# Two-layer encoder: layer 1's feature tiles by seven quarter products, attention without bias tiles, and an empty list of moves

## The chip, the cores and the metric

The kernel runs on one core of a Trainium2 chip (trn2). The metric is the time of one execution on the device, in microseconds; several runs are taken and the median is used. The engines are called PE (matmul), PEld (weight load), DVE (VectorE), ACT (ScalarE), POOL (GpSimd) and SP (the queue that issues most DMAs).

## The reference

The input is 1024 tokens of 1024 features, in float32. Layer 0 has two groups of dense attention (8 heads A, 8 heads B); layer 1, which the change touches, has banded attention. Each layer ends in an output product and a gated residual add. What matters here, cut from the reference (`C_Q` = 1024, `C_KV` = 256, 16 query heads in 4 groups, head size 64, `WINDOW` = 128):

```python
def odd_mixer(h, w_in, sink, w_out, slopes):
    proj = h @ w_in
    qc, kc, vc, gc = jnp.split(proj, [C_Q, C_Q + C_KV, C_Q + 2 * C_KV], axis=-1)
    oc = windowed_sink_attention(qc, kc, vc, sink, slopes)
    return (oc * jax.nn.silu(gc)) @ w_out

# inside windowed_sink_attention, per block of 128 queries and its 3 blocks of keys
bias = -slopes * jnp.abs(rel)
sc = jnp.einsum('bnqkgd,bnskd->bnkgqs', qb, kb) * scale + bias      # -inf outside the band
m = jnp.maximum(jnp.max(sc, axis=-1, keepdims=True), sink_l)
p = jnp.exp(sc - m)
denom = jnp.sum(p, axis=-1, keepdims=True) + jnp.exp(sink_l - m)
```

## The kernel before

Every matmul is done as three: each operand is split into a high part (rounded to the format that PE multiplies fast) and a low part (the rest), and high x high, high x low and low x high are added in PSUM (`mm3`, line 705). So each operand needs a cast (ACT or POOL) and a subtraction (DVE or POOL).

**The order of the work.** The kernel's text does not issue instructions; it records operations in a `Recorder`. A list scheduler (`run`, line 319) then goes through them with a duration for each operation and latencies between engines, and puts on each engine, whenever it is free, the recorded operation with the best priority whose operands are ready and whose buffers can be had. SBUF tiles of 128x1024 float32 come from one pool of `U_BUFS` = 49. `rec.at(shift=...)` lowers a priority, so that filler work goes where nothing else is ready. The list's order is then altered by `MOVES` (line 73), 359 entries of the form (kind, i, j): kind 0 puts operation i, with what it depends on, ahead of j; kind 1 puts i, with what depends on it, behind j (`moved`, line 549). The result is the fixed order in which each engine works.

**The stages,** by the time at which they run in the profiled execution: the input products (to 139 us), heads A in 16 groups with the gate tiles as filler (to 414), heads B in 16 groups (to 642), layer 0's output product and then the entrance of layer 1 (to 759), 32 windows of banded attention with layer 1's feature tiles as filler (to 1053), layer 1's output product (to the end). Groups of heads are numbered 0 to 31, and side work is hung on a group's number: `WS_AT` places sums of weight quarters that DMAs form in DRAM (plain copies on SP, accumulating copies on POOL's queue), `ADA_AT` places blocks of the sums that form shift, scale and gate from the conditioning (`ada_sum`: a 512 KB load and a 128x1024 product-and-sum on DVE, four or eight to a block). The last two blocks stand in the output product of layer 0 (`("op", 1, 7)`) and in a window (`("w", 2, 2)`).

**The output products** of both layers use Winograd's form of Strassen's scheme (`wino_out`, line 1646): 2x2 blocks, seven products instead of eight.

**The feature tiles.** `proj_ft` (line 1847) multiplies one tile of 128 features (2 for keys, 8 for queries, 8 for gates) with one half of the tokens (512): 8 chunks of 128 inputs, three matmuls of 128x512 each, 24 per half. The modulated input of layer 1 lies in `hT1`, 16 tiles for high and low parts of both halves. `fill` takes the next half from a list; six stand ahead of the first window, the others among the windows. Each tile's weights are one load of 512 KB, split on POOL (`wload`, line 873).

**A window** (`win_S`, line 1932, and `win_PV`) takes four heads with the same keys: eight matmuls for the scores, then per head one DVE operation that adds a bias tile (`win_bias`, POOL, four tiles per group of windows) and takes the maximum with the sink's logit, an exponential on ACT with its sum, a division on POOL; between them three small DVE operations and a small exponential for the sink's share. Transposes, splits and the products with the values follow in the next window.

Of the kernel before, what the change touches and what calls it, by code (L numbers as in the profile page):

```python
# [19 lines left out]
P = 128  # L20
# [17 lines left out]
NTAB = 1920  # L38

U_BUFS = 49  # L40
# [29 lines left out]
ADA_AT = (8, 5, ("c2", 6), 2, 4, 10, ("op", 1, 7), ("w", 2, 2))  # L70


MOVES = (
# [60 lines left out]
)  # L134

SLOPES = [float(np.float32(2.0) ** np.float32(-8.0 * k / 16)) for k in range(1, 17)]


class VP:
# [495 lines left out]
def encoder_kernel(ctx: ExitStack, tc: tile.TileContext, xt, ada_t, w_c1, w_c2, w_c3, w_g0, w_uq, w_ukv, w_out0, w_v1,  # L635
# [1211 lines left out]
    def proj_ft(n, name, evac):  # L1847
# [5 lines left out]
        def half(b):  # L1853
            ps = PA(f"{name}{b}")
            for kc in range(KC):
                m_ = mm3(ps, st["w"][kc], hT1[b][kc], kc == 0, kc == KC - 1)
                if kc == 0:
                    first = m_
# [269 lines left out]
```

## Time and profile before

| what | value |
|---|---|
| runs | 1158.09, 1158.74, 1157.87 us; median 1158.09 |
| profiled execution | 1156.2 us from the first to the last instruction (its span; the page gives no other time of it) |
| PE busy | 1129.2 us, 6070 matmuls and transposes |
| DVE / ACT / POOL busy | 924.1 / 697.2 / 592.2 us |
| DMA | 137.64 MB, 119 GB/s on the mean |
| mean granted clock of PE | 0.995 of full speed |

The span is the profiled execution on the chip, first to last instruction; a run's time also holds what lies around that. Busy time of an engine is the time in which one of its instructions was running; matmuls overlap each other, so a busy PE is not yet a PE at its best pace.

### The profile page before, as it was taken

How to read it: one execution, taken by the hardware profiler on the slowest of the kernel's cores; microseconds unless marked ns; L12 is line 12 of the kernel's file. 1: busy time of each engine (PE TensorE's matmuls, PEld its weight loads, DVE VectorE, ACT ScalarE, POOL GpSimd, SP SyncE). 2: the span in 40 equal slices, each digit the busy share in tenths (PEclk: the TensorE clock that was granted, in tenths of full speed). 3: DMA queues.
4: the chain of work that ended last, by engine and by line, in shares of the span. 5: the costliest groups of instructions: out<-in, count | busy, mean ns of one | idle time of the engine just before them, and what ended most of it. 6: DMA issues, size and time to landing. Idle time of an engine off the chain costs nothing.

```text
span 1156.2 us, 17595 instructions
## 1 busy us (share of the span) xinstructions
PE 1129.2 (98%) x6070; PEld 955.9 (83%) x6070; DVE 924.1 (80%) x1662; ACT 697.2 (60%) x1406; POOL 592.2 (51%) x563
## 2 busy tenths in 40 slices
PE   7999999999999999999999999999999999999996
PEld 6898887777788978888888888988888888888885
DVE  7974899898888888888889996858876587766895
ACT  5543366665665787887789823328755466565623
POOL 1235388957875644433436445605465266345524
PEclk9999999999999999999999999999999999999998
DMA  9600466754563251331065335200002112046313
GB/s 367 267 1 30 176 220 199 200 166 153 149 176 92 71 154 51 94 82 50 25 175 209 134 128 191 102 19 19 19 19 92 55 56 92 19 154 247 128 37 146
DMA packets 44617, 137.64 MB, mean 119 GB/s; under 512 B 5488, under 2 KB 8048, under 8 KB 44528
## 3 DMA queue, kind: packets, MB, share of 16 engines
q1 hardware_dynamic: 41648, 127.08, 31.7%
q0 software_dynamic: 2304, 8.39, 4.1%
q8 instruction: 48, 0.79, 0.3%
q10 hardware_dynamic: 576, 1.05, 0.2%
q14 instruction: 41, 0.34, 0.1%
HBM read 105.43 MB, written 39.45 MB: 125 GB/s over the span
## 4 chain that ended last, share of the span: by engine, by line
PE 83%; ACT 4%; DVE 4%; issue 2%; POOL 1%; DMA 1%; SPq 0%; POOLq 0%; ACTq 0%; DVEq 0%
PE psum L612 83%; DVE nm L612 1%; ACT hla L612 1%; ACT Pb L612 1%; ACT Pa L612 1%; DVE hlb L612 1%; ACT hlb L612 1%; DVE hla L612 0%; DMA xr<-in_xt 0%; DVE p L612 0%; ACT q L612 0%; POOL r L612 0%; SPq L612 0%; DVE adag L612 0%; ACT p L612 0%
## 5 line engine op out<-in xcount | busy, mean ns | idle before, releaser
L612 DVE TENSOR_REDUCE nm<-psum 128x1 f32<-128x1024 f32 x128 | 155.1, 1218 | 15.1 <-PE psum L612 13.7
L612 POOL TENSOR_SCALAR p<-p,dn 128x384 f32<-128x384 f32 (+1 forms) x128 | 73.2, 591 | 160.1 <-ACT p L612 71.5
L612 POOL TENSOR_SCALAR Pa<-Pa,rs 128x1024 f32<-128x1024 f32 x64 | 77.0, 1210 | 45.1 <-DVE rs L612 39.6
L612 POOL TENSOR_SCALAR Pb<-Pb,rs 128x1024 f32<-128x1024 f32 x64 | 73.9, 1160 | 44.6 <-DVE rs L612 40.7
L612 PE MATMUL psum<-hla,VA 128*128 128x512 f32 x256 | 89.3, 417 | 3.5 <-DVE hla L612 2.8
L612 DVE TENSOR_TENSOR hla<-psum,hla 128x512 fp32r<-128x512 f32 x128 | 83.9, 683 | 10.6 <-ACT hla L612 10.1
L612 DVE TENSOR_TENSOR hlb<-psum,hlb 128x512 fp32r<-128x512 f32 x128 | 82.7, 684 | 8.9 <-ACT hlb L612 8.4
L612 ACT CAST hla<-psum 128x512 fp32r<-128x512 f32 x128 | 71.2, 594 | 26.9 <-PE psum L612 25.5
L612 PE MATMUL psum<-hlb,VB 128*128 128x512 f32 x256 | 87.3, 422 | 0.1
L612 ACT ACTIVATE Pa<-psum,nm 128x1024 f32<-128x1024 f32 x64 | 71.6, 1120 | 25.3 <-DVE nm L612 21.9
L612 PE MATMUL psum<-ident,Pa 128*128 128x128 f32 x512 | 85.7, 272 | 1.1 <-ACT Pa L612 0.6
L612 PE MATMUL psum<-k,q 128*128 128x512 f32 x256 | 84.1, 402 | 1.6 <-DMA k<-knp 1.1
L612 ACT ACTIVATE Pb<-psum,nm 128x1024 f32<-128x1024 f32 x64 | 71.9, 1124 | 21.0 <-DVE nm L612 14.9
L612 DVE CUSTOM_DVE_ANT_0 p<-psum,bias,rows_g 128x384 f32<-128x384 f32 (+1 forms) x128 | 69.9, 580 | 17.3 <-PE psum L612 16.4
L612 PE MATMUL psum<-ident,Pb 128*128 128x128 f32 x512 | 80.0, 272 | 0.4 <-DVE hlb L612 0.3
L612 ACT COPY ot<-psum 64x512 f32<-64x512 f32 x64 | 37.4, 585 | 69.6 <-PE psum L612 69.1
L612 ACT ACTIVATE p<-p,nm 128x384 f32<-128x384 f32 (+1 forms) x128 | 74.1, 587 | 1.5 <-DVE nm L612 1.5
L612 PEld LDWEIGHTS psum<-ident,Pa 128*128 128x128 f32 x512 | 63.7, 140 | 13.5 <-ACT Pa L612 1.0
L612 ACT CAST hlb<-psum 128x512 fp32r<-128x512 f32 x128 | 69.9, 602 | 5.4 <-PE psum L612 4.6
L612 PEld LDWEIGHTS psum<-ident,Pb 128*128 128x128 f32 x512 | 63.0, 140 | 11.4 <-issue 0.6
L612 ACT CAST hl<-psum 128x512 fp32r<-128x512 f32 x88 | 46.7, 592 | 29.4 <-PE psum L612 28.7
L612 DVE TENSOR_TENSOR hl<-psum,hl 128x512 fp32r<-128x512 f32 x88 | 56.1, 685 | 10.2 <-ACT hl L612 9.7
(891 smaller groups left out, 3596.5 us busy)
## 6 DMA issues: line engine op xcount, KB each, us to landing
ada<-in_ada_t SPq DMA_DIRECT2D x32, 512.0 KB, 7.4
ws<-in_w_out POOLq DMA_DIRECT2D x16, 512.0 KB, 7.3
adag<-in_ada_t SPq DMA_DIRECT2D x16, 512.0 KB, 4.2
S<-ws SPq DMA_DIRECT2D x16, 512.0 KB, 4.4
o<-spill SPq DMA_DIRECT2D x12, 512.0 KB, 5.0
A<-in_w_out SPq DMA_DIRECT2D x12, 512.0 KB, 5.5
xT<-in_xt SPq DMA_DIRECT2D x8, 512.0 KB, 8.4
ws<-in_w_out SPq DMA_DIRECT2D x8, 512.0 KB, 7.7
```

The lines of the kernel that those rows point to most:

```text
L612: fn(*[real(v) for v in a], **{k: real(v) for k, v in kw.items()})
```

## The change

Three things change together.

1. **Seven quarter products for a pair of feature tiles.** The 18 tiles are put in nine pairs (`F_PAIRS`). A pair's weights form a 2x2 of quarters (tile x half of the inputs), the inputs another (half of the inputs x half of the tokens). Four combinations of the weight quarters are formed in DRAM for all pairs, 18 steps at groups 14 to 31 (`feature_sums`: 12 plain copies and 12 accumulating ones of 768 KB). The right-hand combinations are formed once (`combined`) from a float32 copy of the modulated input that `modulate` now writes as well (`keep`), and split into high and low parts: seven operands of four tiles each. `f_step` does one quarter product: 4 chunks x 3 matmuls of 128x512, and what follows it (copies and sums of PSUM banks, or the evacuation of a finished half). Ten of the 63 steps stand ahead of the first window, 53 among the windows. Weights come as pairs of 256 KB quarters, split on POOL (`f_load`); quarter "3" is negated on ACT.
2. **Attention without bias tiles.** Queries are scaled by a power of two of their own and negated; the DVE operation of the scores then takes `relt` (two tables of 384 columns) directly, with a scale and a minimum. The sink's logit is written as one more column of the score tile by POOL, so the exponential's sum holds it. Gone are the bias tiles, the three small DVE operations and the sink's exponential.
3. **The order.** `MOVES` is empty. The last two `ADA_AT` blocks move to groups 18 and 22. `U_BUFS` is 52, and the space that the program reserves for POOL's DMA descriptors is set to 2048.

The diff, cut to its core:

```diff
-U_BUFS = 49
+U_BUFS = 52
-ADA_AT = (8, 5, ("c2", 6), 2, 4, 10, ("op", 1, 7), ("w", 2, 2))
+ADA_AT = (8, 5, ("c2", 6), 2, 4, 10, 18, 22)
-MOVES = (
-    (0, 711, 679), (1, 710, 624), (0, 79, 3), (1, 0, 48), (1, 13, 15), (1, 14, 13), (1, 15, 482), (1, 491, 461),
...
-)
+MOVES = ()
+F_FIRST = ((0, "12"), (1, "12"), (0, "3"), (1, "3"), (0, "6745"), (1, "6745"))
+F_ORDER = "1627543"
+F_EARLY = 10
+FS_AT = tuple((14 + k, k // 6, k % 6) for k in range(18))
...
+            if keep is not None:
+                nc.scalar.activation(keep, src, AF.Identity, bias=sh_col(l, kc))
...
+    def feature_sums(c, step, mark):
...
+            if add:
+                behind(nc.gpsimd.dma_start(out=o, in_=i, accum_op=ALU.add), mark)
+            else:
+                load(o, i, mark)
...
+    def combined():
+        b11, b21, b12, b22 = hf1[0][0:2], hf1[0][2:4], hf1[1][0:2], hf1[1][2:4]
+        nv, ng = nc.vector, nc.gpsimd
+        for eng, o, a, b in ((nv, b22, b12, b22), (nv, b12, b12, b11), (nv, b11, b11, b22), (ng, b21, b21, b11)):
+            for j in range(2):
+                eng.tensor_tensor(out=o[j], in0=a[j], in1=b[j], op=ALU.subtract)
+        T = {}
+        for name, o, eng in (("6", b11, nv), ("7", b22, nv), ("4", b21, ng), ("5", b12, nv)):
+            H, L = two(f"T{name}h"), two(f"T{name}l")
+            for j in range(2):
+                nc.scalar.copy(H[j], o[j])
+                eng.tensor_tensor(out=L[j], in0=o[j], in1=f(H[j]), op=ALU.subtract)
...
+    def f_load(d, mark):
...
+        h, l = UR(f"wf{d}h"), UR(f"wf{d}l")
+        hi_pool(h[:, 0:w], s[:, 0:w])
+        nc.gpsimd.tensor_tensor(out=l[:, 0:w], in0=s[:, 0:w], in1=f(h[:, 0:w]), op=ALU.subtract)
...
+    def f_step():
...
+        for kc in range(4):
+            m_ = mm3(ps, W[kc], TT[p][kc], first and kc == 0, kc == 3, skip_group_check=True)
...
+        if p == "1":
+            nc.scalar.copy(t0, ps)
+        elif p == "2":
+            a(0, ps, 1.0)
+        elif p == "6":
+            nc.vector.tensor_tensor(out=ps, in0=ps, in1=t0, op=ALU.subtract)
+            nc.scalar.copy(t1, ps)
+        elif p == "7":
+            nc.scalar.copy(t0, ps)
+        elif p == "4":
+            b(0, ps, 1.0)
+        elif p == "5":
...
+            nc.vector.tensor_tensor(out=ps, in0=ps, in1=t1, op=ALU.add)
+            b(1, t, 1.0)
+        if n < 2 and p == "5" or n > 1 and p == "3":
+            a(1, ps, -1.0)
...
-                nc.vector.tensor_tensor_reduce(out=pt, in0=s, in1=bias[g, a][:, b * 512 + o:b * 512 + o + n * P], scale=1.0,
-                                               scalar=sinkv[:, j + 4 * g:j + 4 * g + 1], op0=ALU.add, op1=ALU.max,
-                                               accum_out=nm[:, 4 + j:5 + j])
-        nc.vector.tensor_tensor(out=sd, in0=sk, in1=mx, op=ALU.subtract)
-        nc.vector.tensor_scalar_mul(mx, mx, -1.0)
-        nc.scalar.activation(es, sd, AF.Exp)
+                nc.vector.tensor_tensor_reduce(out=pt, in0=s, in1=relt[:, b * 384 + o:b * 384 + o + n * P],
+                                               scale=POW[4 * g + j], scalar=sinkn[:, j + 4 * g:j + 4 * g + 1], op0=ALU.add,
+                                               op1=ALU.min, accum_out=nm[:, j:j + 1])
+            behind(nc.gpsimd.tensor_scalar(col, sinkn[:, 4 * g + 2 * a:4 * g + 2 * a + 2], 1.0, 0.0, op0=ALU.mult, op1=ALU.add),
+                   m_)
...
-        nc.vector.tensor_tensor(out=dn[:, 4:8], in0=dn[:, 0:4], in1=es, op=ALU.add)
-        nc.vector.reciprocal(dn[:, 8:12], dn[:, 4:8])
+        nc.vector.reciprocal(dn[:, 8:12], dn[:, 0:4])
...
+    for _ in range(4):
+        fill()
+    TT = combined()
     for i in range(4, NT):
         v1_tile(i)
+    for _ in range(F_EARLY - 4):
+        fill()
...
+            while f_step.k < F_EARLY + (8 * g + i + 1) * (len(stream) - F_EARLY) // 32:
+                fill()
...
-    nc = bacc.Bacc("TRN2", target_bir_lowering=False, num_devices=1)
+    nc = bacc.Bacc("TRN2", target_bir_lowering=False, num_devices=1, dynamic_dma_scratch_size=2048)
```

More of the change, by code (lines that the diff above doesn't have):

```diff
@@ L1845, in encoder_kernel, with two @@
     Q1 = {}
-    def proj_ft(n, name, evac):
-        st = {}
-        def ld(mark):
-            st["w"] = wload([w_f1[n]], P, f"w{name}", mark=mark, lo_eng="pool")
[L1853 to L1858, printed above, removed]
-            evac(b, ps)
-            return first
-        return ld, half
+    def two(name):
+        return [UR(f"{name}{j}") for j in range(2)]
@@ new lines, in combined @@
+    def combined():
[10 more added lines that the diff above has]
+                eng.tensor_tensor(out=L[j], in0=o[j], in1=f(H[j]), op=ALU.subtract)
+            T[name] = [(H[k // 2][:, (k % 2) * 512:(k % 2 + 1) * 512], L[k // 2][:, (k % 2) * 512:(k % 2 + 1) * 512])
+                       for k in range(4)]
+        T["1"], T["2"], T["3"] = hT1[0][0:4], hT1[0][4:8], hT1[1][4:8]
+        return T
@@ new lines, in encoder_kernel @@
+    stream = [(n, p) for n, ps in F_FIRST for p in ps] + [(n, p) for n in range(2, len(F_PAIRS)) for p in F_ORDER]
+    doubles = {}
+    def f_load(d, mark):
+        if 2 * d >= len(stream) or d in doubles:
+            return
+        todo = stream[2 * d:2 * d + 2]
+        w = 512 * len(todo)
+        s = U(f"wf{d}s")
+        for e, (n, p) in enumerate(todo):
+            kind, *at = F_BLOCK[p]
+            if kind == "A":
+                src = w_f1[at[0], at[1]][:, n * 512:(n + 1) * 512]
+            else:
+                c, (c0, _) = [(c, r) for c, r in enumerate(F_CHUNKS) if r[0] <= n < r[1]][0]
+                src = fs_sp[at[0], c][:, (n - c0) * 512:(n - c0 + 1) * 512]
+            o = s[:, e * 512:(e + 1) * 512]
+            load(o, src, mark)
+            if p == "3":
+                nc.scalar.activation(o, o, AF.Copy, scale=-1.0)
+        h, l = UR(f"wf{d}h"), UR(f"wf{d}l")
+        hi_pool(h[:, 0:w], s[:, 0:w])
+        nc.gpsimd.tensor_tensor(out=l[:, 0:w], in0=s[:, 0:w], in1=f(h[:, 0:w]), op=ALU.subtract)
+        doubles[d] = h, l
@@ new lines, in encoder_kernel @@
+    fbank, fkeep = {}, {}
+    def f_step():
+        k = f_step.k
+        f_step.k += 1
+        n, p = stream[k]
+        a, b = (make_evac[f_[0]](f_[1]) for f_ in F_PAIRS[n])
+        h, l = doubles[k // 2]
+        W = [[t[:, (k % 2) * 512 + kc * P:(k % 2) * 512 + (kc + 1) * P] for t in (h, l)] for kc in range(4)]
+        bank = n, dict(zip("1267453", "XXYYYWZ" if n < 2 else "XXYYYZZ"))[p]
+        first = bank not in fbank
+        if first:
+            fbank[bank] = PA(f"f{n}{bank[1]}")
+        ps = fbank[bank]
+        for kc in range(4):
+            m_ = mm3(ps, W[kc], TT[p][kc], first and kc == 0, kc == 3, skip_group_check=True)
+            if kc == 0:
+                m0 = m_
+        if p == "1":
+            fkeep[n] = U(f"fk{n}")
+        t0, t1 = fkeep[n][:, 0:512], fkeep[n][:, 512:1024]
+        if p == "1":
+            nc.scalar.copy(t0, ps)
[9 more added lines that the diff above has]
+        elif p == "5":
+            if n < 2:
+                nc.vector.tensor_tensor(out=t1, in0=ps, in1=t1, op=ALU.add)
+                t = ps
+                nc.vector.tensor_tensor(out=t, in0=ps, in1=t0, op=ALU.add)
+                ps = fbank[n, "Z"]
+            else:
+                t = PA(f"f{n}W")
+                nc.vector.tensor_tensor(out=t, in0=ps, in1=t0, op=ALU.add)
+            nc.vector.tensor_tensor(out=ps, in0=ps, in1=t1, op=ALU.add)
+            b(1, t, 1.0)
+        if n < 2 and p == "5" or n > 1 and p == "3":
+            a(1, ps, -1.0)
+        if k % 2 == 0:
+            f_load(k // 2 + 2, m0)
+        return m0
@@ L1863, in k_ft, with evac @@
+    f_step.k = 0
     def k_ft(p):
-        def evac(half, ps):
+        def evac(half, ps, sign):
             c = slice(half * 512, half * 512 + 512)
@@ L1871, in evac @@
                 q = slice(64 - e * 64, 128 - e * 64)
-                nc.scalar.copy(kh1[g][r, c], ps[r, :])
-                nc.scalar.copy(kh1[g][q, c], ps[r, :])
+                for x in (r, q):
+                    if sign > 0:
+                        nc.scalar.copy(kh1[g][x, c], ps[r, :])
+                    else:
+                        nc.scalar.activation(kh1[g][x, c], ps[r, :], AF.Copy, scale=-1.0)
             for e in range(2):
@@ L1877, in evac @@
                 q = slice(64 - e * 64, 128 - e * 64)
-                sub(kl1[g][r, c], ps[r, :], f(kh1[g][r, c]))
-                sub(kl1[g][q, c], ps[r, :], f(kh1[g][q, c]))
-        return proj_ft(p, f"k1f{p}", evac)
+                for x in (r, q):
+                    if sign > 0:
+                        sub(kl1[g][x, c], ps[r, :], f(kh1[g][x, c]))
+                    else:
+                        nc.vector.scalar_tensor_tensor(out=kl1[g][x, c], in0=ps[r, :], scalar=-1.0, in1=f(kh1[g][x, c]),
+                                                       op0=ALU.mult, op1=ALU.subtract)
+        return evac
     def q_ft(p):
-        def evac(half, ps):
+        def evac(half, ps, sign):
             Q = Q1[p, half] = UR(f"Q1{p}{half}").rearrange("p (e c) -> p e c", e=2)
@@ L1918, in g_ft_late @@
-        return proj_ft(10 + p, f"g1f{p}", evac)
-    sinkv = rows_g[:, R_SINK:R_SINK + 16]
-    rel = relt
-    bias = {}
-    def win_bias(g):
-        for a in range(2):
-            t = bias[g, a] = U(f"bias{g}{a}")
-            for b in range(2):
-                nc.gpsimd.tensor_scalar(t[:, b * 512:b * 512 + 384], rel, -SLOPES[4 * g + 2 * a + b], 0.0, op0=ALU.mult,
-                                        op1=ALU.add)
+            gated(g1[half][:, (p % 2) * 512:(p % 2 + 1) * 512], ps, sign)
@@ L2031, in encoder_kernel @@
             ada_at(("w", g, i), marks["w", g, i])
-            for _ in range(plan[g][i]):
-                fill(marks["w", g, i - 1] if i else marks.get(("w", g - 1, NT - 1)))
-        if g == 1:
-            fill(marks["w", 1, 7])
-            fill(marks["w", 1, 7])
+            while f_step.k < F_EARLY + (8 * g + i + 1) * (len(stream) - F_EARLY) // 32:
+                fill()
     win_PV(*prev)
-    assert not halves
+    assert f_step.k == len(stream)
     for half in range(2):
@@ L2088, in fts, with pairs @@
         return np.concatenate([chunks(w[:, c:c + P], 8) for c in range(0, w.shape[1], P)])
+    def pairs(w):
+        half = lambda r, c: np.concatenate([w[ft_of(p[r])][:, c * 512:(c + 1) * 512] for p in F_PAIRS], 1)
+        return np.ascontiguousarray(np.stack([np.stack([half(r, c) for c in range(2)]) for r in range(2)]))
     ada_t = np.ascontiguousarray(i["ada_w"].transpose(0, 2, 1)).reshape(48, P, 1024)
```

98 lines of the change are left out of this document (56 added, 42 removed), and 59 rows, old and new, of the table MOVES.

## The prediction

> **What bounds the kernel now.** I read the page first (busy shares, clock), then a table of busy times by stage, the chain that ended last, the list of TensorE's waits, and last the rows of single operations. A row of an operation has line, engine, operation, tiles out<-in, shapes and count, then busy us and mean ns, then the idle time before it.
>
> ```profile
> span 1156.2 us, 17595 instructions
> PE 1129.2 (98%) x6070; PEld 955.9 (83%) x6070; DVE 924.1 (80%) x1662; ACT 697.2 (60%) x1406; POOL 592.2 (51%) x563
> ```
>
> TensorE is busy for 1129.2 of 1156.2 us, and no other engine comes near. I cut the span where the kernel changes its work: start, heads A, heads B, layer 0's output product with the entrance of layer 1, banded attention with the feature tiles as filler, layer 1's output product.
>
> ```profile
> core 0: us, PE busy (x) PEld busy (x) DVE busy (x) ACT busy (x) POOL busy (x), PEclk, DMA share, GB/s
> 0.00:139.00 139.00, 130.80 (x736) 118.00 (x737) 103.36 (x158) 64.83 (x143) 47.59 (x46) 1.00 0.44 171
> 139.00:414.00 275.00, 269.55 (x1466) 221.12 (x1465) 241.79 (x381) 178.20 (x329) 198.21 (x192) 0.99 0.55 162
> 414.00:642.00 228.00, 225.88 (x1267) 188.28 (x1267) 193.57 (x307) 181.54 (x334) 102.60 (x85) 1.00 0.33 99
> 642.00:759.00 117.00, 117.00 (x616) 100.53 (x615) 95.78 (x123) 49.98 (x70) 57.59 (x30) 1.00 0.37 132
> 759.00:1053.00 294.00, 293.13 (x1529) 249.98 (x1529) 213.77 (x596) 175.52 (x461) 141.67 (x177) 1.00 0.17 59
> 1053.00:1156.00 103.00, 92.88 (x464) 77.95 (x462) 75.80 (x102) 47.14 (x72) 44.50 (x33) 0.96 0.37 135
> ```
>
> So where the change removes matmuls (642 to 1053) TensorE idles 0.9 us in 411, at the full granted clock, with DVE at 82% and 73%. Time taken from TensorE there is time taken from the span, as long as the others keep up. The chain says the same: from 615 to 854 us it never leaves TensorE.
>
> ```profile
> by line: PE psum L612 82.7%; issue 1.6%; DVE nm L612 0.8%; ACT hla L612 0.7%; ACT Pb L612 0.6%; ACT Pa L612 0.6%; DVE hlb L612 0.5%; ACT hlb L612 0.5%; DVE hla L612 0.5%; DMA xr<-in_xt 0.4%; DVE p L612 0.4%; ACT q L612 0.4%; POOL r L612 0.3
> 615.37 238.98 PE psum L612 x1277
> ```
>
> **The seven products.** Before, 18 feature tiles x 2 halves x 8 chunks x 3 matmuls = 864 of 128x512. After, 63 quarter products x 4 chunks x 3 = 756. So 108 go: 24 before the first window (6 halves of 24 become 10 products of 12) and 84 among the windows. Their pitch is read from starts, since a matmul's own 0.39 us overlaps its neighbours:
>
> ```profile
> 803.26 0.48 PE L612 MATMUL psum<-hT11l,wq1f2h 128*128 128x512 f32 x1
> 803.58 0.39 PE L612 MATMUL psum<-hl,V 128*128 128x512 f32 x1
> 805.88 0.39 PE L612 MATMUL psum<-hT11h,wq1f2h 128*128 128x512 f32 x1
> 807.72 0.39 PE L612 MATMUL psum<-hT11h,wq1f2l 128*128 128x512 f32 x1
> ```
>
> Eight pitches (nine filler matmuls) from 805.88 to 807.72 give 0.230 us. 108 x 0.230 = **-24.8 us**. The first two rows show a stall too short for any list: 0.32 instead of 0.23, so 0.09 us lost.
>
> **The other engines among the windows.** The sums, copies, weight splits and small operations have these rows (DVE, then ACT, then POOL):
>
> ```profile
> L612 DVE TENSOR_TENSOR psum<-psum,sa 128x512 f32<-128x512 f32 x4 | 2.8, 693 | 0.3 <-PE psum L612 0.3
> L612 DVE TENSOR_SCALAR nm<-nm 128x4 f32<-128x4 f32 x32 | 7.9, 250 | 0.6
> L612 DVE TENSOR_TENSOR nm<-rows_g,nm 128x4 f32<-128x4 f32 x32 | 6.4, 200 | 0.4
> L612 DVE TENSOR_TENSOR dn<-dn,nm 128x4 f32<-128x4 f32 x31 | 5.5, 178 | 10.9 <-ACT p L612 10.6
> L612 DVE CUSTOM_DVE_ANT_0 adag<-adag,cb,g 128x1024 f32<-128x1024 f32 x8 | 11.2, 1410 | 0.0
> L612 ACT COPY sa<-psum 128x512 f32<-128x512 f32 x4 | 2.4, 590 | 0.3 <-PE psum L612 0.3
> L612 ACT ACTIVATE nm<-nm 128x4 f32<-128x4 f32 x32 | 6.5, 208 | 21.2 <-DVE nm L612 21.2
> L612 POOL TENSOR_TENSOR wq1f2l<-wq1f2s,wq1f2h 128x1024 fp32r<-128x1024 f32 x1 | 2.4, 2411 | 0.1
> L612 POOL TENSOR_SCALAR wq1f2h<-wq1f2s 128x1024 fp32r<-128x1024 f32 x1 | 1.1, 1056 | 0.0
> L612 POOL TENSOR_SCALAR p<-p,dn 128x384 f32<-128x384 f32 x96 | 57.3, 616 | 64.9 <-DVE dn L612 40.4 <-DVE nm L612 8.1 <-ACT a111h L612 7.0
> L612 POOL TENSOR_SCALAR p<-p,dn 128x256 f32<-128x256 f32 x28 | 14.1, 521 | 91.4 <-ACT p L612 71.0 <-DVE dn L612 10.4 <-ACT ot L612 5.3
> L612 POOL TENSOR_SCALAR bias<-relt 128x384 f32<-128x384 f32 x16 | 8.2, 517 | 1.0
> ```
>
> Of 63 products 53 fall here, so 53/7 x 3 = 23 sums and 23 copies. DVE: + 23 x 0.693 = 16, - (7.9 + 6.4 + 5.5) for three small operations per window, - 4 x 1.41 for an ada block moved away: 213.8 becomes 204. ACT: + 23 x 0.59 + 8 negations at about as much - 6.5: 175.5 becomes 187. POOL: 27 weight pairs instead of some 15 tiles, + 12 x (2.41 + 1.06) = 42; 64 writes of the sink column, bounded by 0 and 0.52, on the line through 616 and 521 at 128 columns apart about 0.33, + 21; - 8.2 of bias: 141.7 becomes 196. TensorE's own need is 293.1 - 19.3 = 274. DVE at 74%, ACT at 68%, POOL at 71% of that: all hidden. ACT's exponential now also waits for POOL's column, which can stand behind one 2.41 us split; the list puts a whole window (274 / 32 = 8.6 us of TensorE) between scores and their transposes. I take 0; if that cover goes, the fourth rival prices it.
>
> **The entrance (642 to 759).** The right-hand combinations: three differences of two tiles each and three splits of two on DVE, 12 operations of 128x1024; one difference and one split on POOL, 4 operations; 8 casts and 16 more copies on ACT, which has room (50 of 117). Moved away: the other ada block.
>
> ```profile
> L612 DVE TENSOR_TENSOR t10l<-t,t10h 128x1024 fp32r<-128x1024 f32 x2 | 4.6, 2322 | 0.0
> L612 DVE TENSOR_TENSOR s10l<-S,s10h 128x1024 fp32r<-128x1024 f32 x2 | 2.3, 1212 | 0.0
> L612 DVE CUSTOM_DVE_ANT_0 adag<-adag,cb,g 128x1024 f32<-128x1024 f32 x4 | 6.1, 1537 | 0.0
> L612 POOL TENSOR_TENSOR a220l<-A,a220h 128x1024 fp32r<-128x1024 f32 x2 | 5.9, 2986 | 1.7 <-ACT a220h L612 1.7
> L612 DVE TENSOR_TENSOR t10l<-t,t10h x2: 1215/2322/3428, 673.8 to 680.6; 128x1024 fp32r<-128x1024 f32 x2
> ```
>
> TensorE's need falls to 117.0 - 24 x 0.23 = 111.5. DVE's is 95.8 - 6.1 + 12 x 1.21 + 4 x 0.69 = 107 at the short duration, and 95.8 - 6.1 + 12 x 2.32 + 2.8 = 120 at the long one. So between 0 and 9 us of TensorE's time go here; nearer the lower end, since the third quarter product and the last four V tiles need nothing of it: **+3**. The two equal t10l operations took 1.22 and 3.43 us, the second while POOL ran its a220l. The Trainium skill, "SBUF — State Buffer", section "SBUF: two separate sides", has a rule for that: a DVE operation with two SBUF inputs and a GpSimd operation share one port pair, and whichever is second is blocked for the whole of the first. The trace agrees (3.43 - 1.22 = 2.2, about a POOL operation's length); by that rule all twelve could stand at the long duration, and the entrance would cost the 9, the third rival's time.
>
> **Heads B.** Two ada blocks land here (groups 18 and 22): 8 x 1.41 = 11 us more of DVE, with their 8 loads on SP; also 12 plain copies on SP and 12 accumulating copies of 768 KB on POOL's queue.
>
> ```profile
> L612 POOL DMA_DIRECT2D ws<-in_w_out x16 | 14.1, 970 | 0.0
> PE psum L612 <- DMA k<-knp: 1.1, 1, 1.1
> ws<-in_w_out SPq DMA_DIRECT2D x8, 512.0 KB, 7.7
> ```
>
> POOL: 12 x 0.97 = 12 us on 102.6 of 228, hidden. SP: one of those copies, 7.7 us x 1.5, may stand ahead of the small k and q moves, for which TensorE waits 1.1 us once today; at worst four more such waits. DVE goes from 85% to 90%, where heads A (88%) already leave 2.0% of TensorE idle against 0.9% here. At A's share B would idle 4.5 instead of 2.1: **+2.4**, between 0 and 7.
>
> **Buffers.** The seven right-hand operands hold 28 tiles instead of 16 until the last pair, with 52 tiles instead of 49. The trace has no such wait; a late weight pair costs at most its preparation, 3.5 us. Between 0 and 7 (two such), nearer the lower: **+2**.
>
> **The emptied list.** All 359 entries of MOVES go; the order is what the planner's list gives. By the time at which the named instruction runs, 179 entries lie in heads A, 83 in heads B, 60 among the windows, 4 in the entrance, 33 at start and end. The entrance, hardly touched, idles 0.00: the list alone can fill TensorE where DVE has room. Heads A and B idle 7.6 us even with 262 entries. A gain is left out: the four stages from 139 to 1053 idle 8.4 us together, all that any order could win there. Upper end: each entry a stall of the 0.09 us seen above, 359 x 0.09 = 32. I take the bare idle of A and B as twice today's, + 7.6; the windows' as twice, + 0.9; start and end 33 x 0.09 = + 3.0: **+11.5**, nearer the lower end because of the entrance's row.
>
> **Sum.** - 24.8 + 3 + 2.4 + 2 + 11.5 = - 5.9 on a span of 1156.2: 1150.3. The runs' median, 1158.09, is 1.9 above the span of the profiled execution; with that, **1152**.
>
> **Rivals.** First, the list is as good everywhere as in the entrance: order at 0, buffers at 0, entrance 1: 1158.1 - 24.8 + 1 + 2.4 = 1137. For it: 0.00 idle in that row; against: heads A. Second, and on the other side: the order eats the gain. Its place is heads A and B, its price above 24.8 - 7.4 = 17.4 turns the sign, and at 32 the time is 1173; 1167 stands for it. For it: 262 entries there, DVE at 88 and 85%; against: the waits view finds few waits to undo.
>
> ```profile
> PE psum L612 <- DVE hla L612: 3.0, 3, 1.5
> PE psum L612 <- ACT Pa L612: 1.8, 3, 0.8
> ```
>
> Third, the entrance becomes DVE's: 9 instead of 3, 1158, no difference. Fourth, fewer filler matmuls leave the windows waiting for their own chain, and the 19.3 us saved there come back as idle: 1171. Against it: TensorE's 0.87 us of idle in 294 today, and no other engine above 74% after.
>
> **Chances.** Forecast 0.38, first rival 0.12, second 0.30, third 0.12, fourth 0.08. Faster by over 0.2% (2.3 us, about what a measurement here can tell from none): 0.50; within: 0.12; slower: 0.38. The range reaches from the first rival to the second's end, 1137 to 1174; the likeliest case's own is 1143 to 1156.
>
> **What would show it.** TensorE with 5962 matmuls and about 25 us less need; idle in heads A near 11 and in heads B near 7 us; the windows' stage near 275 us with TensorE still over 98%; an entrance near 115 us, with DVE's 128x1024 rows between 1.2 and 3.4 us. Idle in A and B above 20 us together makes the second rival; TensorE below 95% among the windows the fourth. The forecast fails most easily by the order's price, the one term that no row measures.

## The result, and the profile after

The changed kernel takes 1169.0 us in the median of four runs (1163.7 to 1171.3), against 1158.15 for the kernel before beside it: a ratio of 1.0091, 95% interval 1.0074 to 1.0109. It is 0.9% slower, where 1152 and a gain had been forecast. The head of its page, and two of its rows in 40 equal slices, for TensorE and for the granted clock:

```profile
span 1169.5 us, 17544 instructions
PE 1123.8 (96%) x5962; PEld 942.4 (81%) x5962; DVE 950.9 (81%) x1607; ACT 731.0 (63%) x1434; POOL 671.2 (57%) x656
PE   7999999999999999999989899998999999999996
PEclk8999999999999999999989999998999999999998
```

The 108 matmuls are gone (5962 for 6070), yet TensorE's busy time fell by 5.4 us only, and the span grew by 13.3. Between its start and its end the PE row has three dips, in the slices that begin at 585, 643 and 789 us. The first and the last are repeated in the row of the granted clock. The table of busy times by stage, cut where the stages' first matmuls run (layer 0's output product and the entrance are apart here):

```profile
core 0: us, PE busy (x) PEld busy (x) DVE busy (x) ACT busy (x) POOL busy (x), PEclk, DMA share, GB/s
0.00:139.00 139.00, 132.22 (x732) 120.06 (x733) 102.97 (x156) 64.89 (x142) 49.11 (x47) 0.98 0.44 169
139.00:428.00 289.00, 279.00 (x1508) 227.01 (x1507) 246.35 (x391) 183.09 (x340) 207.63 (x198) 0.99 0.61 174
428.00:663.00 235.00, 226.48 (x1229) 185.48 (x1229) 198.73 (x316) 177.97 (x326) 109.59 (x91) 0.99 0.62 177
663.00:737.00 74.00, 74.00 (x332) 60.93 (x330) 59.30 (x70) 34.89 (x45) 32.36 (x16) 1.00 0.37 132
737.00:805.00 68.00, 63.38 (x364) 55.21 (x364) 55.32 (x74) 37.22 (x67) 45.25 (x25) 0.97 0.16 52
805.00:1066.00 261.00, 257.49 (x1354) 217.93 (x1353) 204.65 (x504) 185.60 (x445) 177.82 (x246) 0.99 0.23 79
1066.00:1169.00 103.00, 91.28 (x454) 75.75 (x452) 83.60 (x103) 47.32 (x73) 49.45 (x36) 0.97 0.40 142
```

Read the counts before the lengths. Heads A grew from 275 to 289 us, but hold 42 matmuls more (1508 for 1466), and heads B 38 fewer: the list has moved work across the boundary. The same goes for the entrance and the windows. So only sums are compared: heads A and B together went from 503 to 524, layer 1 (entrance and windows) from 337 to 329, about 8 us gained where 22 were forecast.

Then the clock. Over the whole execution its mean is 0.987, against 0.995 before: 1169.5 x 0.013 = 15.2 us lost, against 5.8. Of these, 3.0 and 4.0 cost nothing: in both traces the last stretch at half clock (5.9 and 7.9 us, to the end of the span) lies behind the last matmul. What is left, some 12 us against 2, stands in the table nearly all as busy time, not as idle. A hole in heads B shows how it arises, by four adjoining stretches of 3.41 us and by TensorE's timeline:

```profile
590.16:593.57 3.41, 3.41 (x23) 2.78 (x21) 2.02 (x4) 3.34 (x8) 0.00 (x0) 1.00 0.85 143
593.57:596.99 3.42, 0.29 (x2) 0.00 (x0) 1.89 (x3) 2.69 (x6) 0.00 (x0) 1.00 1.02 226
596.99:600.40 3.41, 2.63 (x6) 1.79 (x7) 0.00 (x0) 0.00 (x0) 0.00 (x0) 0.50 1.08 293
600.40:603.81 3.41, 3.41 (x14) 2.73 (x13) 2.16 (x3) 0.93 (x2) 0.00 (x0) 0.50 0.99 339
```

```profile
593.38 0.48 PE L566 MATMUL psum<-k,q 128*128 128x512 f32 x1
597.77 0.76 PE L566 MATMUL psum<-k,q 128*128 128x512 f32 x1 [3.91 <-issue]
```

TensorE stands still for 3.91 us before a score matmul. The trace names no releaser ("issue"); I take it that its q arrives late: all DMA engines are taken (share 1.02), after POOL had issued an accumulating copy of 768 KB at 589 us, and without the sums' DMAs, in the same order, this wait is gone (run `a_nosum` below). Then the clock is 0.50 for 6.8 us, and where 23 matmuls fitted in a stretch, 14 do.

### The profile page after: what moved, and what is told of

The parts are those of the page before. It is cut to its first block, busy times and chain, and to the rows that moved or that the text cites. A ratio compares the mean times of both kernels' runs of the same rounds, so it can differ in the third digit from the quotient of the medians.

```text
span 1169.5 us, 17544 instructions
## 1 busy us (share of the span) xinstructions
PE 1123.8 (96%) x5962; PEld 942.4 (81%) x5962; DVE 950.9 (81%) x1607; ACT 731.0 (63%) x1434; POOL 671.2 (57%) x656
## 3 DMA queue, kind: packets, MB, share of 16 engines
q10 hardware_dynamic: 576, 1.05, 0.2%
## 4 chain that ended last, share of the span: by engine, by line
PE 78%; DVE 12%; ACT 3%; DMA 3%; issue 2%; POOL 1%; SPq 0%; POOLq 0%; ACTq 0%; DVEq 0%
PE psum L566 78%; DVE nm L566 2%; DMA A<-in_w_out 1%; DVE psum L566 1%; DVE p L566 1%; ACT Pa L566 1%; DVE hlb L566 1%; DMA xr<-in_xt 1%; DVE Q L566 1%; DMA xT<-in_xt 1%; POOL r L566 1%; DVE adag L566 1%; ACT hla L566 1%; DMA o<-spill 0%; DVE o L566 0%
## 5 line engine op out<-in xcount | busy, mean ns | idle before, releaser
L566 POOL TENSOR_SCALAR Pb<-Pb,rs 128x1024 f32<-128x1024 f32 x64 | 77.6, 1216 | 49.8 <-DVE rs L566 40.9
L566 POOL TENSOR_SCALAR Pa<-Pa,rs 128x1024 f32<-128x1024 f32 x64 | 79.9, 1254 | 41.6 <-DVE rs L566 33.2
L566 POOL TENSOR_SCALAR p<-p,dn 128x384 f32<-128x384 f32 (+1 forms) x128 | 70.8, 570 | 47.0 <-DVE dn L566 44.5
L566 PE MATMUL psum<-hla,VA 128*128 128x512 f32 x256 | 91.8, 422 | 5.1 <-DVE hla L566 4.2
L566 DVE TENSOR_TENSOR hla<-psum,hla 128x512 fp32r<-128x512 f32 x128 | 83.2, 681 | 10.6 <-ACT hla L566 10.2
L566 DVE CUSTOM_DVE_ANT_0 p<-psum,relt,sinkn 128x384 f32<-128x384 f32 (+1 forms) x128 | 69.8, 579 | 13.4 <-PE psum L566 11.4
L566 ACT ACTIVATE p<-p,nm 128x385 f32<-128x385 f32 (+1 forms) x128 | 74.7, 590 | 9.4 <-POOL p L566 6.2
L566 PEld LDWEIGHTS psum<-ident,Pb 128*128 128x128 f32 x512 | 63.7, 142 | 16.7 <-POOL Pb L566 2.7
```

What stands on the lines that cost most here:

```text
L566: fn(*[real(v) for v in a], **{k: real(v) for k, v in kw.items()})
```

## Experiments

Theory 1, after the result: the gain of the seven products is there, and the order and the clock give it back. Rivals: the added work (sums by DMA, the two moved ada blocks, the combinations) costs it in whatever order; or the emptied list cost the same on any kernel and the added work the rest. All ratios are to the kernel before, run beside. The median of that kernel lay between 1156.2 and 1158.2 us from one set of runs to the next, so a difference in us between two sets is good to some 2 us.

### The bare list alone (`b_bare`)

```diff
-MOVES = (
...
-)
+MOVES = ()
```

> The kernel before with an empty list of moves and nothing else changed. Theory 1 (the order is what the change lost): heads A lengthen from 275 to about 289 us and heads B from 228 to some 232, as they did in the changed kernel, and the whole is about 1178 us, so that bare against bare the change gains some 9 us. The prediction's own price of the order, 11.5 us, would give 1170. Theory 2 (the lost time comes from what the change adds to heads A and B: DMA sums, two ada blocks, other buffers): the time stays within 4 us of 1158. In both, the product of span and mean granted clock should grow less than the span, if stalls of 1 to 4 us are followed by 3.4 us at half the clock as in the changed kernel's trace.

Measured: 1170.67 us, ratio 1.0116 (1.0100 to 1.0131). On the kernel before, the 359 entries are worth 13.5 us, near the prediction's own price. From this bare kernel to the changed one the change brings only 1.7 us, by the ratios 2.9, where theory 1 had some 9.

### The sums' DMAs alone, in the old order (`b_sums`)

```diff
+                for call in self.extra.get(o.i, ()):
+                    call()
```

> The kernel before with its moves kept, plus the 24 DMAs that form the weight combinations in DRAM at groups 14 to 31 (their results are not used). Theory 1 (order): no change beyond 2 us. Theory 2 (the sums delay the small k and q moves of heads B, for which TensorE waits): one or more holes of some 4 us in heads B, each with 3.4 to 6.8 us at half the clock behind it, so 3 to 8 us more, and a wider spread of the runs.

Measured: 1172.65, ratio 1.0134 (1.0117 to 1.0151): 15 us, for DMAs whose results nothing uses, nearly twice the upper end of what theory 2 expected. Waits of TensorE, and the small moves' time to landing:

```profile
PE psum L613 <- DMA q<-qr_sp: 5.7, 1, 5.7
PE psum L613 <- DMA k<-knp: 5.5, 3, 2.8
```

```profile
k<-knp SPq DMA_DIRECT2D x32, 128.0 KB, 6.1
```

The k move lands after 6.1 us (the same row of the kernel before has 2.3). In an order fitted without the copies, TensorE stands still four times for small moves, 11.2 us in all. The stretch in which the longest wait begins, and the 10.2 us after it:

```profile
413.90:417.50 3.60, 0.18 (x1) 0.00 (x0) 1.48 (x4) 1.91 (x5) 2.45 (x3) 0.99 1.09 276
417.50:427.70 10.20, 5.13 (x11) 3.64 (x12) 1.61 (x2) 0.97 (x2) 0.00 (x0) 0.50 1.05 250
```

DMA share 1.05 to 1.09, and the clock at 0.50 for three steps.

### Taking the added work out of the changed kernel, order fixed (`a_nosum`, `a_noada`, `a_nocomb`, `a_t4`, `a_none`)

```diff
-                behind(nc.gpsimd.dma_start(out=o, in_=i, accum_op=ALU.add), mark)
+                rec.dropped.add(behind(nc.gpsimd.dma_start(out=o, in_=i, accum_op=ALU.add), mark).i)
...
+            rec.dropped.add(ld.i)
+            rec.swapped[tr.i] = (tc.nc.vector.tensor_copy, (o, first), {})
...
-                eng.tensor_tensor(out=o[j], in0=a[j], in1=b[j], op=ALU.subtract)
+                rec.dropped.add(eng.tensor_tensor(out=o[j], in0=a[j], in1=b[j], op=ALU.subtract).i)
...
+                    rec.swapped[lo.i] = (tc.nc.gpsimd.tensor_scalar, (L[j], o[j], 1.0, 0.0), dict(op0=ALU.mult, op1=ALU.add))
...
+                    rec.swapped[lo.i] = (tc.nc.vector.tensor_copy, (L[j], o[j]), {})
```

Without the sums' DMAs:

> The changed kernel in the very same order, without the 24 DMAs that form the weight combinations; the products that use them read plain weight quarters of the same size instead, so the output is not the reference's. Theory 2: the 3.9 us hole in heads B is gone, heads B shrink from 235 to about 229 us, and the time falls to 1161 to 1163 with a spread below 2 us. Theory 1: the hole is one of the order's, and the time stays at 1164 to 1171.

Without the two ada blocks:

> The changed kernel in its own order, with the two ada blocks of heads B (groups 18 and 22) left out: their 8 loads dropped, their 8 sums on VectorE replaced by copies of one column, so layer 1's gate is not the reference's. If VectorE's 11 us there cost TensorE time (the prediction gave 2.4 us), heads B shrink by 2 to 4 us and the time falls to 1165 to 1167. If the rest of heads A and B is lost to the order alone, the time stays within 2 us of the changed kernel's 1169.

Without the combinations:

> The changed kernel in its own order, with the right-hand combinations cheapened: the eight differences are left out, and the eight splits become copies with one input on the same engines, so the output is not the reference's. Theory E (the entrance of layer 1 waits for VectorE, whose operations with two SBUF inputs and POOL's stand in each other's way): entrance and first windows lose their holes and the half-clock stretches behind them, entrance and windows together fall from 329 to about 319 us, the time to 1158 to 1161. Rival (the quarter products are poor filler for the windows, whatever the entrance does): less than 3 us.

POOL's two splits with one input instead of two:

> The changed kernel in its own order, where only POOL's two splits of the fourth product's operand become copies with one input (about 1.05 us instead of 2.9 each); the output is not the reference's. VectorE's T6 split took 3.08 us behind them instead of 1.22. If that one collision holds the entrance, 2 to 5 us go; if VectorE's queue itself does, less than 1 us.

All three parts out:

> The changed kernel in its own order without all three: no DMA sums, no ada blocks in heads B, cheap right-hand combinations; the output is not the reference's. If the three costs are separate they add up: 5.6 us for the sums as measured, 2 to 4 for the ada blocks, 8 to 11 for the combinations, so 1149 to 1153, about 20 us below the kernel before with an empty list of moves (1170.7), which would be most of the 24.8 us of matmuls. If they hide one another: 1157 or more.

| left out | us | ratio (95%) | off the changed kernel | mean clock, profiled run |
|---|---|---|---|---|
| sums | 1163.38 | 1.0047 (1.0030 to 1.0063) | 5.6 | 0.990 |
| ada blocks | 1164.91 | 1.0069 (1.0054 to 1.0084) | 4.1 | 0.992 |
| combinations | 1161.31 | 1.0036 (1.0022 to 1.0050) | 7.7 | 0.989 |
| one collision on POOL | 1168.38 | 1.0092 (1.0071 to 1.0114) | 0.6 | 0.989 |
| all three | 1157.15 | 0.9997 (0.9988 to 1.0006) | 11.9 | 0.994 |

The three add up to 17.4, and together they are worth 11.9. That does not show that they share holes: each difference is taken from the same changed kernel, whose four runs lie between 1163.7 and 1171.3 us, so its error counts three times in the sum. By the ratios it is 14.0 against 10.9. Much of each difference is the clock's. Span times mean clock, the time at full clock, falls by 4.3 us without the sums, 0.9 without the ada blocks, 4.0 without the combinations and 6.1 without all three; the clock takes the rest (for all three 8.3 of the 14.4 us between the two profiled executions: 15.2 lost before, 1155.1 x 0.006 = 6.9 after). And not all of that is the left-out work's doing. Two stretches at half clock of the changed kernel, at 16.7 and 255.7 us, are missing without the ada blocks of heads B, which run only behind 428 us. So of the prediction's 2.4 us for these blocks this run shows nothing clear.

What it does show: even with all of the added work gone the bare kernel only ties with the kernel before. But bare against bare, 13.5 us below `b_bare`, more than half of the 24.8 us of matmuls then come out. The collision with POOL is there in the rows, yet taking it away is worth 0.6 us, nothing by the ratio, so it alone doesn't hold the entrance. In the entrance (timelines of POOL, DVE and TensorE) DVE's T6l takes 3.08 us and T7l 2.00, the first while POOL runs its two T4l, the second beside POOL's wf5h (1.22 us is what such a split takes alone, as T6l and T7l do at 780.7 and 772.6 us). TensorE waits for what DVE does after each, a Q and, as I read the rows, through ACT's fk a sum:

```profile
784.12 5.74 POOL L566 TENSOR_TENSOR T4l<-xr,T4h 128x1024 fp32r<-128x1024 f32 x2
784.54 3.08 DVE L566 TENSOR_TENSOR T6l<-xr,T6h 128x1024 fp32r<-128x1024 f32 x1
788.39 0.39 PE L566 MATMUL psum<-kh,Q 128*128 128x256 f32 x1 [1.59 <-DVE Q L566]
790.14 1.05 POOL L566 TENSOR_SCALAR wf5h<-wf5s 128x1024 fp32r<-128x1024 f32 x1
790.26 2.00 DVE L566 TENSOR_TENSOR T7l<-xr,T7h 128x1024 fp32r<-128x1024 f32 x1
793.54 0.50 PE L566 MATMUL psum<-T7h,wf3h 128*128 128x512 f32 x1 [2.21 <-ACT fk L566]
```

### The ada blocks back in their old places (`a_ada`)

```diff
-ADA_AT = (8, 5, ("c2", 6), 2, 4, 10, 18, 22)
+ADA_AT = (8, 5, ("c2", 6), 2, 4, 10, ("op", 1, 7), ("w", 2, 2))
```

> The changed kernel with the last two ada blocks at their old places, the entrance of layer 1 and a window, instead of groups 18 and 22. The planner makes its list anew, so some of the difference is a new order. If the blocks in heads B cost what the prediction gave (2.4 us), heads B shrink by 2 to 3 us and the entrance and windows grow by as much or more, as DVE has 6 us more to do there: within 3 us of the changed kernel, 1166 to 1172.

Measured: 1191.47, ratio 1.0297 (1.0281 to 1.0313), far from what I expected. The list is made anew here, and entrance and windows took 354 us instead of 329. The run tells nothing of the blocks' own cost, since order and place change together, and it made me suspect the order itself.

### An order of its own, and the control (`a_moves`, `b_moves`, `a_moves2`)

```diff
-MOVES = ()
+MOVES = (
+    (1, 2363, 2324),
+    (0, 2335, 2246),
...
+)
```

The changed kernel, 439 entries:

> The changed kernel with an order of its own: MOVES filled with 439 entries, found by putting off the operation for which TensorE would next stand still or drawing forward what it waits for, with room left for transfers that come late. Nothing else is edited. Theory 1 (the 24.8 us of matmuls are there to be had, and it is the order, not the added work, that gives them back): 1141 to 1151, 18 to 28 below the changed kernel; heads A near 275, heads B near 229, entrance with windows near 320. Rival (the added work itself costs some 17 us in whatever order; a good order is worth the 13.5 us that it was worth to the kernel before): 1153 to 1158, a tie with the kernel before.

The kernel before, 385 new entries found in the same way:

> The control: the kernel before, its own 359 entries of MOVES replaced by 385 that are found from its bare list in the very way of the run above. If the new entries are merely as good as the old ones: 1153 to 1161, and what the changed kernel gains on it with an order of its own is the change's. Rival (the new way of ordering is the better one, and any gain above is its doing): 1146 or less, and then only the difference to the run above belongs to the change: theory 1 has that at 8 to 14 us.

The changed kernel again, 301 other entries:

> The changed kernel with another order found in the same way from another starting seed, with less room left for late transfers (301 entries). If the exact order hardly matters once it is fitted: within 4 us of the run with 439 entries. If the room for late transfers is what counts (the copies of 768 KB hold up the small moves): 5 to 12 us slower than it, with TensorE waiting for DMAs of k and q.

Measured: 1148.37 (ratio 0.9929, 0.9913 to 0.9944), 1156.33 (1.0000, 0.9991 to 1.0009) and 1143.49 (0.9887, 0.9869 to 0.9906). The control ties, so the new way of ordering is no better for the old kernel than its own entries. The changed kernel gains 20.6 and 25.5 us by it (18.7 and 23.6 by the ratios), and with 301 entries is 1.1% faster than the kernel before: the version that beats both. My rival on room for late transfers failed: the order with less room is the faster. The comparison isn't quite even. The changed kernel had two orders, and the control was made as the first of them: against that one the change gains 8.0 us, against the second 12.8. Whether an order with less room would help the kernel before as well was not tried.

Four kernels, each in two rows: both heads' stages, then entrance and windows. First before and after with the bare list, then before and after with an order found for each (columns as above):

```profile
138.10:649.10 511.00, 499.57 (x2736) 408.78 (x2735) 438.51 (x689) 359.59 (x663) 299.87 (x277) 1.00 0.45 132
722.90:1063.70 340.80, 338.13 (x1815) 289.08 (x1815) 253.38 (x649) 191.81 (x489) 166.79 (x192) 1.00 0.20 67
```

```profile
139.10:662.90 523.80, 505.27 (x2735) 412.29 (x2733) 444.89 (x706) 360.88 (x666) 317.22 (x289) 0.99 0.62 175
736.80:1065.60 328.80, 320.67 (x1715) 272.82 (x1714) 259.76 (x577) 222.62 (x510) 222.87 (x270) 0.99 0.22 73
```

```profile
136.30:641.50 505.20, 499.04 (x2755) 413.28 (x2753) 437.08 (x693) 359.46 (x663) 303.67 (x277) 1.00 0.45 134
713.40:1052.50 339.10, 336.57 (x1815) 290.40 (x1814) 254.20 (x648) 192.16 (x489) 166.28 (x193) 1.00 0.20 67
```

```profile
137.50:647.30 509.80, 499.16 (x2745) 410.55 (x2743) 446.39 (x707) 361.21 (x666) 317.44 (x289) 1.00 0.63 180
719.00:1038.90 319.90, 317.45 (x1716) 270.88 (x1716) 255.31 (x576) 222.83 (x509) 223.36 (x270) 1.00 0.23 75
```

With the bare list the change costs 12.8 us in the heads and brings 12.0 in layer 1. With fitted orders it costs 4.6 and brings 19.2. The changed kernel's work is the same in both orders (DVE 444.89 and 446.39 in the heads, POOL 317.2 and 317.4), only its place differs, and the last kernel's clock is 1.00 in both rows.

### The sums once more, in fitted orders (`a_mvnosum`, `a_mv2nosum`)

The order of 439 entries, then that of 301, each without the sums' DMAs (edit as above).

> The changed kernel in the order of the run with 439 entries, held fixed, without the 24 DMAs that form sums of weight quarters (12 copies, 12 accumulating copies); the products that need sums read plain quarters of w_f1, so their values differ. If the sums' DMAs cost by standing ahead of small moves in any order: 4 to 8 us below that run, as with the bare list (5.6). If a fitted order hides them: within 2 us of it.

> The changed kernel in the order with 301 entries, without the 24 DMAs of the sums of weight quarters; the products that need sums read plain quarters, so their values differ. If the 4.6 us found in the order with 439 entries were mostly the clock's (17 us at half pace there against 7 without the sums): under 2 us below 1143.5. If the copies themselves delay what TensorE waits for: 4 to 6 us below, 1138 to 1140.

Measured: 1143.76 (0.9889, 0.9874 to 0.9904), which is 4.6 below its kernel; and 1142.96 (0.9879, 0.9863 to 0.9895), 0.5 below its own, within its spread. So in the second order the copies cost nothing that can be told. The 4.6 in the first were the clock's: 0.989 with the sums and 0.994 without, 12.6 us lost against 6.9. More than half of that isn't the copies' doing: ahead of 341 us, where the first copy is issued, the trace with the sums has 13.6 us at half clock and the one without 6.8, which is 3.4 us of the loss.

### Holes, long and short (`h_long`, `h_short`)

```diff
+                if o.i in self.holes:
+                    for _ in range(6):
+                        self.nc.scalar.copy(real(kw["rhs"]), real(kw["rhs"]))
...
+                if l == 0 and (name, u) in [('6', 0), ('7', 0), ('4', 0), ('5', 0), ('3', 0)]:
+                    rec.holes.add(marks["wino", l, name, u].i + 2)
```

This is `h_long`; `h_short` has `range(1)` and all four parts (0 to 3) of the five products.

> The changed kernel in the order with 301 entries (1143.5 us, no stretch at half clock), with five holes put into layer 0's output product, where TensorE never idles: in five of the seven products, ahead of the third matmul, ACT copies that matmul's moving operand onto itself six times, and TensorE waits for it. Values are unchanged. Each hole is estimated at 3.3 us from ACT's 0.59 us rows. If standing still costs only its own length: 17 us more, about 1160. If the clock is halved after it, each hole costs one or two stretches of 3.4 us at half pace besides, 1.7 to 3.4 us: 1169 to 1177, with the granted clock of that stage near 0.85.

> The same with twenty holes of one copy each, one in each of the four parts of those five products: about 0.75 us each, 15 us in all, so nearly the stillness of the five long holes. If standing still costs only its length, both theories agree: 1156 to 1161, the granted clock of that stage 1.00. If the clock is lost by the sum of stillness, however cut up, it would lose as much here as with the long holes: above 1167.

Measured: 1175.52 (ratio 1.0157, 1.0134 to 1.0180) and 1161.48 (1.0037, 1.0023 to 1.0052), which is 32.0 and 18.0 above the kernel without holes; 30.0 and 15.2 of it lie in the stage with the holes. Layer 0's output product without holes; with five long ones (and three rows of TensorE's timeline at one of them: the pitch after it is 0.42 us); with twenty short ones:

```profile
647.30:719.00 71.70, 71.70 (x322) 59.38 (x321) 59.52 (x70) 35.17 (x46) 33.13 (x16) 1.00 0.39 136
```

```profile
649.80:751.50 101.70, 82.90 (x323) 66.11 (x322) 60.24 (x72) 54.38 (x79) 33.55 (x17) 0.88 0.28 96
```

```profile
676.11 0.50 PE L872 MATMUL psum<-t20h,s20l 128*128 128x512 f32 x1 [3.79 <-ACT t20h L871]
677.22 0.63 PE L872 MATMUL psum<-t20h,s20h 128*128 128x512 f32 x1
677.64 0.63 PE L872 MATMUL psum<-t20l,s20h 128*128 128x512 f32 x1
```

```profile
647.70:734.60 86.90, 76.92 (x322) 58.08 (x321) 59.10 (x70) 45.23 (x65) 35.02 (x17) 1.00 0.33 112
```

Five holes of 3.8 us lengthen the stage by 30.0: 18.8 of idle (101.70 - 82.90) and 11.2 of busy time at half pace (82.90 - 71.70), 2.2 for each hole. Twenty short ones lengthen it by 15.2 at clock 1.00. (The page's idle is 10.0 there, since the last matmul before each hole counts as busy to its end.) So standing still in pieces of 3.8 us halves the clock for a while, and in pieces of some 0.76 us, spread over the stage, it doesn't. It is also why the hole at 594 us of the changed kernel costs more than its length.

## Why the prediction was wrong

**The step that failed** is the sum itself: the price of the emptied list, 11.5, was taken from the old work and added to the change, as if each had its own price, and the clock stood in the sum at nothing. For the old work the price was good: 13.5 measured, and 8.0 of it in the heads (511.0 for 503), where 7.6 had been forecast. The changed kernel pays 25.5 for the same lack (1169.0 less 1143.5; 23.6 by the ratios), since its added DMAs fall where the list leaves no slack (the hole at 594 us goes with them), and since holes are long enough to halve the clock. That its added DVE work does the same is not shown.

In terms: span times mean clock, time at full clock, is 1150.4 before, 1164.0 for the bare list, 1154.3 after. (Each is good to 1 or 2 us, as the mean clock has three digits and takes in the stretch behind the last matmul.) So of the 13.3 us of span + 13.6 are the order (forecast 11.5), - 9.7 the change (forecast - 24.8 + 7.4 = - 17.4), + 9.4 the clock (forecast 0). The clock is the largest part of the miss of 19.2, and the change's other terms are 7.7 of it.

1169 lies inside the stated range, and the chance of a slower kernel had been put at 0.38; the likeliest case, its sign and its size were wrong.

**The clock** had no term. Its sign stood in rows that I had quoted: a clock of 0.99 in heads A, and a wait for hla whose longest was 1.5 us. After that very wait (1.51 us, to 231.8) the kernel before runs one step of 3.4 us at half clock, its only one between the start and the last matmul. I read the waits' sum, not their length.

**Seven products.** The - 24.8 for the matmuls holds nearly, for a good order: with fitted orders layer 1 falls by 19.2, where - 24.8 with + 3 for the entrance had promised 21.8.

**Heads B** (2.4) **and buffers** (2). With fitted orders the heads cost 4.6 us more, 4.4 was forecast: the sum of the two terms fits a good order, but no run tells them apart. With the bare list it is 12.8, near the upper ends of both terms together. The one wait I named for it, a copy ahead of the small moves, is nearly what the hole at 594 us shows. I had expected it from a plain copy on the queue of the small moves, and it came beside an accumulating one on POOL's queue; I gave it a microsecond and it took 3.9, and nearly twice that with the clock (6.8 us at half clock).

**Entrance** (3, to 9). Measured with the windows, since filler moved across: taking the combinations out gave 7.7 with the bare list (6.4 between the profiled executions, 4.0 of it at full clock: 1154.3 less 1163.1 x 0.989). It did not become DVE's as a whole: DVE is busy 55 of 68 us.

**What would show it.** Idle of heads A and B was forecast as 11 and 7 and is 10.0 and 8.5, so by my own sign (above 20 together) the second rival had not come true. In effect it had: the order ate the gain, at 1169 for its 1167. The sign missed it, because much of the loss is busy time at half pace. That the two times agree is partly luck. The rival wanted a price above 17.4 for the list alone, which was 13.5, and it put the loss into heads A and B: of what the order of 301 entries gives back 14.0 us lie there (523.8 to 509.8) and 8.9 in entrance and windows (328.8 to 319.9). The windows' stage came out at 261 instead of 275 and the entrance with the output product at 142 instead of 115, both by filler that the list drew forward (696 matmuls in the latter, where 592 were to be left). The windows ran at 98.7% busy, so the fourth rival was rightly low.

**What stays open.** Fitted, the two kernels differ by 12.8 us, while the terms without the order gave 17.4. In both traces the one stretch at half clock that is recorded lies behind the last matmul, so the clock isn't the reason. The missing 4.6 lie in layer 1 (19.2 for 21.8), in the heads (4.6 for 4.4), and 1.8 in the remaining stages, for which there was no term. Which part of the added work holds them wasn't tried in a fitted order, beyond the sums.

## What to carry to other kernels

A change to a kernel whose order is fitted by hand is two changes: measure the old kernel in the bare order and the new one in an order of its own before judging it, and read stages by their matmul counts, since a list moves work across boundaries. Price a wait by its length, not only by the sum of waits: several short ones that lie apart are cheaper than a long one, as the long one takes the clock with it (here from somewhere between 1.35 and 1.95 us of idle within one step of 3.41). And leave DMAs of 768 KB out of the time in which a 128 KB move is awaited, or order the work with them in view.

## What the runs showed of the hardware that I had not expected

**The clock is decided on a fixed grid.** In the seventeen traces the granted clock changes only in steps of 3.413 us from the first change on, and is 1.0 or 0.5. Counting over all steps that ran at full clock, up to the last matmuls of each trace: of 30 with more than 1.95 us of TensorE idle all were followed by a step at half clock; of 5553 with less than 1.35 us none; of 57 between, 15. An early one, from heads A of the kernel after:

```profile
252.30:255.71 3.41, 1.50 (x10) 1.08 (x9) 3.37 (x5) 3.36 (x6) 0.56 (x1) 0.99 1.05 274
255.71:259.12 3.41, 3.41 (x10) 2.65 (x9) 2.03 (x4) 1.99 (x5) 2.93 (x3) 0.51 1.03 299
```

One gap of 1.91 us, and the next step is at half pace. So what counts is the idle time within one step, and where a gap falls on the grid decides. The wait for t21l in layer 1's output product shows it: 2.16 us long in the changed kernel, it is cut by the grid, the fuller step holds 1.77 us of idle, and the clock stays at 1.00. Without the ada blocks (`a_noada`) it is 2.14 us long and lies in one step, and the next, from 1099.8 us, is at 0.50. The Trainium skill, "TensorE: Matmul & The Clock Gate", section "Part 1: The HAM clock gate (the "warmup" mystery)", has a free-running window of 3413 ns and two clocks; the traces agree with both. Its section "HAM oscillation — how this bites in real kernels" gives as the rule no idle gaps above about 3.4 us; here the measurement differs, for gaps of 1.9 us were enough when they fell inside one step. The grid may also make the spread between runs of the changed kernel, though no run tests it: its four runs have spans of 1161.9 to 1169.5 at clocks of 0.993 to 0.987, and the product of the two is 1153.8 to 1155.0 in all. It isn't so for every kernel: the control's ten runs have spans of 1153.9 to 1156.1 and products of 1146.7 to 1152.4.

**Large copies delay small moves, on another queue too.** With the sums' DMAs a k move's landing went from 2.3 us (kernel before) to 4.1; without them, in the same order, it is 2.3 again (`a_nosum`). Half of these copies are issued on POOL's queue and half on SP's, which also issues the k and q moves. At the hole of 594 us it was POOL's: from 571 to 598.9 us SP's queue issues k and q moves alone.

```profile
fs<-in_w_f POOLq DMA_DIRECT2D x12, 768.0 KB, 8.1
k<-knp SPq DMA_DIRECT2D x32, 128.0 KB, 4.1
```

In the fitted order with 301 entries it is still 4.0, and costs little: there TensorE waits for a k move once, for 0.5 us.
